# Finer regions in an ordering model: quarters of the inverse's DRAM tiles and buffers, halves of stored weights, columns of tables

## The chip, the core and the metric

The kernel runs on one core of one Trainium2 chip. The metric is the device time of one execution in microseconds. Beside it stands one execution that the hardware profiler recorded: its timeline runs from the first to the last instruction (the "span"), and it names for each group of instructions the engine, the output tile and the input tiles. The engines are PE (matrix products), PEld (PE's weight loads, which overlap it), DVE, ACT and POOL (work on rows of SBUF and PSUM), and SP, which here only issues DMAs; "SPq" is its queue. "Granted clock" is the share of PE's full speed that the profile shows as granted.

## What is computed

One decoder layer on 4096 tokens of width 1024, followed by an RMSNorm. One projection of the normalised input feeds two head groups: four heads of gated linear attention (GLA) and eight RWKV-7 heads. Their outputs, gated, are concatenated, projected and added to the input.

```python
def _rwkv7_scan(r, decay, k, v, kk, a):
    def step(S, inp):
        r_t, w_t, k_t, v_t, kk_t, a_t = inp
        sa = jnp.einsum('bhvk,bhk->bhv', S, -kk_t)
        S = (S * w_t[:, :, None, :]
             + sa[..., None] * (kk_t * a_t)[:, :, None, :]
             + v_t[..., None] * k_t[:, :, None, :])
        y = jnp.einsum('bhvk,bhk->bhv', S, r_t)
        return S, y
...
def _hybrid_layer(x, norm_w, w_in, ...):
    h = _rmsnorm(x, norm_w)
    u = (h @ w_in).astype(f32)
    gla_u, rwkv_u = u[..., :GLA_IN], u[..., GLA_IN:]
...
    o = _gla_chunked(q, k, v, log_a.reshape(B, T, GLA_HEADS, GLA_DK))
...
    y = _rwkv7_scan(r_h, decay.reshape(hs), k_h, v_h, kk, a.reshape(hs))
...
    merged = jnp.concatenate([gla_out, rwkv_out], axis=-1).astype(x.dtype)
    return x + merged @ w_out
```

The state S of an RWKV head is corrected at every token by a rank-one term that depends on S itself. The kernel takes 64 tokens at a time; within such a chunk the corrections form a triangular system, whose matrix it inverts.

## The kernel before

**Tiling.** The tokens are cut into 8 blocks of 512. In a block, the 8 RWKV heads are worked in 4 pairs; a pair in a block is a "unit", 32 in all, numbered 4 x block + pair. A unit has 8 chunks of 64 tokens. Tiles hold features on the 128 partitions and tokens along the row, so that the two heads of a pair fill the two halves of 64 partitions. Activations and weights of the large projections are split into a high and a low f16 part, and the products run as matmuls of 128x512 (`bank<-x,wr`, `bank<-x,wg`, `bank<-x,wo`).

**Streams.** Eight generators are interleaved: x (load and normalise a block), w (load the 37 weight tiles, scale them, split them into f16 halves, store each into its own DRAM tile `wdr`; the first twelve also stay in SBUF), a (`rwkv_ab`, line 862: the projections of r, k, v and the gate of a unit, on buffers `wr`), i (`rwkv_i`, line 1012), c (`rwkv_c`, line 1034), p and g (the GLA heads, on buffers `wg`) and o (`out_block`, line 1272, and `out_last` for the last block, on buffers `wo`). Both halves of a stored weight are loaded again into a `wr`, `wg` or `wo` buffer for each use: 256 KB a transfer. `absmax_scale`, with its small tile `amo`, scales the merged heads before the output projection.

**The inverse of a unit.** After the projection of r, PE makes the score products `bank<-DD,bk` (32 for a unit), and DVE copies the lower triangles into the tile `Nb`, which holds for each chunk a 128x128 square for the two heads. The square's four diagonal blocks of 32x32 are inverted on POOL, all chunks and blocks of a unit at once, with the 32 blocks laid on 128 partitions. For that layout the blocks go through DRAM and back:

```python
        F = sb(rt, [P, 1024], F32, "f4", 1).rearrange("p (k t) -> p k t", k=32)
        nd = sb(dr, [4, NC, 32, 32], F32, "nd", 2)
        for q in range(4):
            D.dma_start(nd[q].rearrange("c j i -> j c i"), nb[32 * q:32 * q + 32, :, 32 * q:32 * q + 32])
        for g in range(4):
            D.dma_start(F[32 * g:32 * g + 32].rearrange("p k t -> p (k t)"), nd.rearrange("q c j i -> (q c) (j i)"))
...
        td = sb(dr, [8, 4, 32, 32], F32, "td", 2)
        for g in range(4):
            D.dma_start(td[:, g].rearrange("m q i -> q m i"), Tc[32 * g:32 * g + 32])
        for q in range(4):
            D.dma_start(nb[32 * q:32 * q + 32, :, 32 * q:32 * q + 32],
                              td[:, :, NC * q:NC * q + NC].rearrange("m g c i -> (m g) c i"))
```

Four stores fill `nd`, a quarter each. Four loads fill `F` (in the profile "f"); each reads all of `nd` and writes 32 partitions. Between the two pieces shown, POOL solves in 31 steps of two operations on `tm` and `Tc` (DVE in the last unit). Four stores fill `td`, and four loads put the inverted blocks back into `Nb`, 32 partitions each. Then `rwkv_i` transposes (tile `Ta`) and joins the 32x32 blocks into the inverse of 64x64 by the products `bank<-Ta,Nb` and `bank<-Nb,Ta`.

**The chain.** `rwkv_c` walks the 8 chunks of a unit in turn. Each has three products that wait for one another through ACT and DVE: `ch<-sv,DD`, `ch<-us,Nb`, `ch<-uv,bk`. The y products follow. A unit's chain needs the state that the chain of the same pair left in the block before, and the chains run one after the other.

**The order.** No instruction is issued as the generators come to it. Every call of an engine passes through a helper (`Engine.call`; all instructions have its line, 438, in the profile), which gives it a modelled duration and a lag, and hands it to `put` (line 223). `put` builds a graph: a step follows the last writer of each region that it reads or writes, and the readers of each region that it writes. A follower waits in the model for the end and the lag of the step before, if the region is "timed", that is, if `parts` (line 105) names it too; otherwise only its place behind that step is kept. A DMA that stores into `nd` or `td` has a lag of 0.6 or 1.2 us, and `SPARE` adds 0.45 behind each DMA. The first pass (`account`, line 169) interleaves the streams by these times, with the same regions. Then `forward` and `backward` (lines 264 and 332) place all steps on modelled engines, in 50 passes with five settings, and the pass whose modelled end is smallest sets the order in which all instructions are issued. SP has one queue for all DMAs, in that order. What an instruction waits for on the chip does not come from this model but from its real operands.

**Regions.** `whole` (line 203) gives the regions of an operand. Before, a DRAM tile is one region, and so is a table named in `TABLES` (small tiles in which each column belongs to another weight or pair); an SBUF tile has one region for each half of 64 partitions, and some are cut further by their row. So in the model the four stores into one `nd` follow each other, each after the one before has landed; the same holds for `td`, and for the steps that write different columns of one table.

Of the kernel before, what the change touches and what calls it, by code (L numbers as in the profile page):

```python
# [18 lines left out]
DRAM = bass.MemoryType.DRAM  # L19

P = 128
DM = 1024
KT = 8
# [23 lines left out]
NC = TB // C  # L47
# [34 lines left out]
def hymba_kernel(ctx, tc, xT, wt, wg, wo, wua, gup, pk, ck, out):  # L82
# [14 lines left out]


    TABLES = ("pkt", "scl", "invs", "hinv", "mu_s", "omu_s", "carry", "wosc", "woinv", "gnh", "lnh")
    HEADS, XS = set(), set()  # L100
    now = [0.0]
    streams = []
    ready, used, busy = {}, {}, {}

    def parts(ap):
        if ap.tensor.name == out.tensor.name or ap.tensor.name.rsplit("_", 1)[0] in TABLES:
            return []
        if ap.space == DRAM:
            return [(ap.tensor.name, 0)]
        a = ap.start_partition()  # L110
        hs = range(a // 64, (a + ap.shape[0] - 1) // 64 + 1)
        if ap.tensor.name in HEADS:
            o = ap.offset % P // 64
            e = range(2) if ap.ap[-1][1] > 64 else range(o, o + 1)
            return [(ap.tensor.name, h, i) for h in hs for i in e]
        if ap.tensor.name in XS:
            o = ap.offset % (4 * TB) // TB
            e = range(o, o + max(1, math.prod(ap.shape[1:]) // TB)) if ap.dtype == F16 else range(4)
            return [(ap.tensor.name, h, 2 + i) for h in hs for i in e]
        return [(ap.tensor.name, h) for h in hs]  # L120
# [48 lines left out]
    def account(eng, out, ins, d, lag, cols=0, tiles=None):  # L169
        rdy = lambda k: (lambda r: r[0] + early(r[1], eng))(ready.get(k, (0.0, "")))  # L170
        t = max([0.0] + [rdy(k) for a in ins for k in parts(a)]
                + [used.get(k, 0.0) for k in parts(out)]
                + [rdy(k) for k in parts(out) if eng != "T"])
        if eng == "T":
            t0, d = array.put(max(t, now[0]), d, cols, tiles)
            t, now[0] = t0, array.free
        else:
            if eng == "D":
                t0 = place("H", t, 0.5)
                t = t0 + 1.15  # L180
            t = place(eng, t, d)
            if eng != "D":
                t0 = t
        for a in ins:
            for k in parts(a):
                used[k] = max(used.get(k, 0.0), t + d + (0.95 if eng == "D" else 0.1))
        for k in parts(out):
            ready[k] = (t + d + lag, eng)
        return t0
# [13 lines left out]
    def whole(ap):  # L203
        if ap.tensor.name == out.tensor.name:
            return []
        if ap.tensor.name.rsplit("_", 1)[0] in TABLES or ap.space == DRAM:
            return [(ap.tensor.name, 0)]
        return parts(ap)

    class Step:  # L210
# [12 lines left out]
    def put(t0, eng, d, lag, cols, tiles, tab, outs, ins, f):  # L223

        keys = lambda aps: {k: k in {y for x in aps for y in parts(x)} for a in aps for k in whole(a)}
        ki, ko = keys(ins), keys(outs)
        for k in list(ki) + list(ko):
# [250 lines left out]
    def sb(pool, shape, dt, tag, bufs=1):  # L478

        key = (tag, dt)  # L480
        if key not in ring:
            ring[key] = [0, [pool.tile(shape, dt, tag=f"{tag}_{i}", name=f"{tag}_{i}") for i in range(bufs)]]
        r = ring[key]
        t = r[1][r[0] % len(r[1])]
        r[0] += 1
        return t
# [32 lines left out]
    for g in range(4):  # L519
        q = slice(32 * g, 32 * g + 32)  # L520
# [38 lines left out]
    Nb = [sb(un, [P, NC, 192], F32, f"Nb{i}") for i in range(NBUF)]  # L559
# [37 lines left out]
    wdr = [dr.tile([2, P, KT, P], F16, tag=f"wdr{i}", name=f"wdr{i}") for i in range(NWT + KT)]  # L597
# [987 lines left out]
```

## Time and profile before

| | |
|---|---|
| median of 3 runs | 2355.93 us (2353.73 to 2357.6) |
| the profiled execution | 2350.84 us |
| its span | 2348.7 us |
| mean granted clock of PE | 0.982 |
| PE busy | 2230.6 us |
| HBM read, written | 276.94 MB, 45.05 MB |

The profiled execution is one of its own, a little shorter than the three timed runs; its own time is 2.1 us more than its span. Three groups of matmuls make up two thirds of PE's busy time; columns are the line, engine, operation, output and inputs, tile and shape, type and count, then busy us and mean ns of one, then the idle time of the engine before them and what ended it:

```
L438 PE MATMUL bank<-x,wr 128*128 128x512 f16 x3264 | 795.7, 381 | 13.3 <-DVE SC L438 4.7
L438 PE MATMUL bank<-x,wg 128*128 128x512 f16 x1536 | 376.9, 381 | 1.9 <-ACT bk L438 1.2
L438 PE MATMUL bank<-x,wo 128*128 128x512 f16 x1488 | 364.2, 382 | 2.2 <-DMA wr<-wdr 0.8
```

The mean of one matmul there is its own length; matmuls overlap, so that the pace at which they follow each other is read from a run of them in a timeline. Idle time is credited in such rows to the group that stands behind it, and the releaser is inferred from semaphores.

### The profile page before, as it was taken

The page shows a single profiled execution, that of the slowest core. Times are in us where ns is not written, and L with a number is a line of the kernel's source. Part 1 is how long each engine was busy: PE and PEld are TensorE (multiplying, and loading weights), DVE is VectorE, ACT ScalarE, POOL GpSimd, SP SyncE. Part 2 cuts the span into 40 slices and gives each one's busy share as a digit, 9 for nine tenths or more (in the row PEclk, how much of TensorE's full clock was granted, in tenths as well). Part 3 has the DMA queues.
Part 4 walks back from the last instruction along what each step waited for, and adds up shares of the span by engine and source line. Part 5 has one row for each costly group of instructions (what it writes and reads, how often), then busy time and mean ns, then how long its engine had stood idle before and what let it go on. Part 6 is the DMA issues. An engine that isn't in the chain of part 4 may idle for free.

```text
span 2348.7 us, 52029 instructions
## 1 busy us (share of the span) xinstructions
PE 2230.6 (95%) x19304; PEld 1365.0 (58%) x19304; DVE 1715.9 (73%) x3801; ACT 1257.4 (54%) x3229; POOL 865.6 (37%) x2212
## 2 busy tenths in 40 slices
PE   6998999899999999999999999999999999999976
PEld 2555565456665557556575556655575565755643
DVE  7977778568773886849776687748867487766756
ACT  7557765345643646545654556446464555544442
POOL 2442333524334153444524253341524446241300
PEclk9988999999999999999999999999999999999989
DMA  5685645354334642445434543346424464344432
GB/s 183 199 267 167 187 151 151 93 175 139 111 105 128 191 147 74 127 128 188 131 92 124 184 145 109 106 127 192 148 76 128 121 193 121 98 119 123 123 96 75
DMA packets 275362, 325.41 MB, mean 139 GB/s; under 512 B 131572, under 2 KB 132772, under 8 KB 275108
## 3 DMA queue, kind: packets, MB, share of 16 engines
q1 hardware_dynamic: 275108, 322.10, 45.5%
q8 instruction: 151, 2.47, 0.4%
q14 instruction: 103, 0.84, 0.1%
HBM read 276.94 MB, written 45.05 MB: 137 GB/s over the span
## 4 chain that ended last, share of the span: by engine, by line
PE 72%; DVE 14%; DMA 7%; ACT 4%; issue 2%; SPq 1%; POOL 0%; DVEq 0%; ACTq 0%; POOLq 0%
PE bank L438 63%; PE ch L438 7%; PE y L438 3%; DVE DD L438 1%; DMA wg<-wdr 1%; SPq L438 1%; DVE bk L438 1%; DVE x L438 1%; DMA rn<-bcda 1%; DVE nta L438 1%; DMA xr<-in_xT_dram 1%; ACT wo L438 1%; DVE Nb L438 1%; DMA wdr<-wo 1%; DVE mgr L438 1%
## 5 line engine op out<-in xcount | busy, mean ns | idle before, releaser
L438 PE MATMUL bank<-x,wr 128*128 128x512 f16 x3264 | 795.7, 381 | 13.3 <-DVE SC L438 4.7
L438 POOL TENSOR_TENSOR tm<-Tc,f 128x60 f32<-128x60 f32 (+24 forms) x961 | 338.3, 352 | 583.1 <-DMA f<-nd 468.1
L438 PEld LDWEIGHTS <-wr 128*128 128x128 f16 x3264 | 314.1, 100 | 314.7 <-issue 25.6
L438 POOL TENSOR_TENSOR Tc<-Tc,tm 128x60 f32<-128x60 f32 (+24 forms) x961 | 356.7, 371 | 74.6
L438 PE MATMUL bank<-x,wg 128*128 128x512 f16 x1536 | 376.9, 381 | 1.9 <-ACT bk L438 1.2
L438 PE MATMUL bank<-x,wo 128*128 128x512 f16 x1488 | 364.2, 382 | 2.2 <-DMA wr<-wdr 0.8
L438 DVE SCALAR_TENSOR_TENSOR sv<-ch,PC,psd 64x64 f32<-64x64 f32 x448 | 126.5, 282 | 217.2 <-PE ch L438 212.1
L438 POOL TENSOR_TENSOR xacc<-xacc,xr 128x512 f32<-128x512 f32 x98 | 132.7, 1354 | 344.2 <-ACT xr L438 229.5
L438 PEld LDWEIGHTS <-wg 128*128 128x128 f16 x1536 | 147.7, 100 | 149.3 <-issue 8.1
L438 PEld LDWEIGHTS <-wo 128*128 128x128 f16 x1488 | 146.2, 101 | 133.5 <-issue 4.9
L438 PE MATMUL bank<-wg,x 128*128 128x128 f16 x3072 | 197.5, 222 | 12.4 <-DMA wg<-wdr 12.3
L438 PEld LDWEIGHTS <-x 128*128 128x128 f16 x3120 | 189.6, 100 | 32.3 <-issue 20.0
L438 ACT ACTIVATE psd<-sv,PC 128x128 f32<-128x128 f32 x256 | 102.3, 400 | 180.7 <-DVE sv L438 135.2
L438 ACT COPY uv<-ch 64x64 f32<-64x64 f32 x512 | 105.8, 207 | 106.7 <-PE ch L438 100.8
L438 POOL MEMSET Tc<- 32x8 f32 (+1 forms) x160 | 23.6, 148 | 360.1 <-DMA td<-Tc 312.2
L438 ACT COPY us<-ch 64x64 f32<-64x64 f32 x512 | 105.5, 206 | 91.7 <-PE ch L438 83.5
L438 PEld LDWEIGHTS ch<-sv,DD 128*128 128x128 f32 x512 | 91.5, 192 | 41.4 <-DVE sv L438 14.9
L438 PEld LDWEIGHTS ch<-uv,bk 128*128 128x128 f32 x512 | 91.1, 192 | 41.5 <-ACT uv L438 16.1
L438 PEld LDWEIGHTS ch<-us,Nb 128*128 128x128 f32 x512 | 88.6, 192 | 44.7 <-ACT us L438 21.5
L438 ACT ACTIVATE sa<-bank,mu_s 128x512 f32<-128x512 f32 x104 | 71.6, 688 | 75.1 <-PE bank L438 74.3
L438 PE MATMUL ch<-uv,bk 128*128 128x128 f32 x512 | 105.8, 289 | 5.5 <-ACT uv L438 5.2
L438 PE MATMUL ch<-sv,DD 128*128 128x128 f32 x512 | 105.2, 288 | 4.9 <-DVE sv L438 4.7
(333 smaller groups left out, 3681.7 us busy)
## 6 DMA issues: line engine op xcount, KB each, us to landing
wr<-wdr SPq DMA_DIRECT2D x256, 256.0 KB
wg<-wdr SPq DMA_DIRECT2D x184, 256.0 KB
xr<-in_xT_dram SPq DMA_DIRECT2D x176, 256.0 KB
wo<-wdr SPq DMA_DIRECT2D x128, 256.0 KB
f<-nd SPq DMA_DIRECT2D x128, 128.0 KB
x<-in_wt_dram SPq DMA_DIRECT2D x29, 512.0 KB
wdr<-wo SPq DMA_DIRECT2D x25, 512.0 KB
out_dram<-mgg SPq DMA_DIRECT2D x33, 256.0 KB
```

The source lines that it names most:

```text
L438: put(t0, self.name, d, lag, cols, tiles, tab, outs, ins, lambda: f(*a, **kw))
```

## The change

The table of regions becomes finer. A new function `dram` gives four regions for a tile `nd` (a store touches the one that it writes, a load into F touches all four), four for `td` (again a store touches one, a load back into `Nb` all four) by their offsets, two for a stored weight `wdr` (the high and the low f16 half), and one for any other DRAM tile. `Nb` and `f` have a region for each 32 and each 16 partitions instead of 64. A table has a region for each column of its row; as before, tables are not timed.

The diff:

```diff
@@ -97,17 +97,33 @@
     TABLES = ("pkt", "scl", "invs", "hinv", "mu_s", "omu_s", "carry", "wosc", "woinv", "gnh", "lnh")
+    FINE = {"Nb": 32, "f": 16}
     HEADS, XS = set(), set()
...
+    def dram(ap):
+
+        name = ap.tensor.name
+        if name.startswith("nd"):
+            return [(name, i) for i in (range(4) if ap.shape[0] == 32 and len(ap.shape) == 2 else [ap.offset // (NC * 1024) % 4])]
+        if name.startswith("td"):
+            return [(name, i) for i in (range(4) if ap.ap[0][0] >= 1024 else [ap.offset // 1024 % 4])]
+        if name.startswith("wdr"):
+            return [(name, i) for i in ([ap.offset // (P * DM) % 2] if ap.ap[0][1] == P and len(ap.shape) == 3 and ap.shape[1] == KT and ap.shape[2] == P else range(2))]
+        return [(name, 0)]
+
     def parts(ap):
         if ap.tensor.name == out.tensor.name or ap.tensor.name.rsplit("_", 1)[0] in TABLES:
             return []
         if ap.space == DRAM:
-            return [(ap.tensor.name, 0)]
+            return dram(ap)
         a = ap.start_partition()
+        tag = ap.tensor.name.rsplit("_", 1)[0].rstrip("0123456789_")
+        if tag in FINE:
+            q = FINE[tag]
+            return [(ap.tensor.name, h) for h in range(a // q, (a + ap.shape[0] - 1) // q + 1)]
         hs = range(a // 64, (a + ap.shape[0] - 1) // 64 + 1)
@@ -203,8 +219,11 @@
     def whole(ap):
         if ap.tensor.name == out.tensor.name:
             return []
-        if ap.tensor.name.rsplit("_", 1)[0] in TABLES or ap.space == DRAM:
-            return [(ap.tensor.name, 0)]
+        if ap.space == DRAM:
+            return dram(ap)
+        if ap.tensor.name.rsplit("_", 1)[0] in TABLES:
+            w = math.prod(ap.tensor.shape[1:])
+            return [(ap.tensor.name, i) for i in range(ap.offset % w, ap.offset % w + math.prod(ap.shape[1:]))]
         return parts(ap)
```

The number of instructions of each kind is the same; the order differs on all five engines, nearly everywhere. (The lines are shifted: what was line 438 is line 457.) Three places, as the two programs issue them, follow; a number behind a tile's name is its buffer, and x4 stands for four in a row.

SP's queue in unit 10, from its first store into `nd` to its loads of F (`f_0_215`); `xr`, `wr` and `bcdx`, `xacc` are loads and broadcasts of other streams. Before:

```order
L438 DMA nd_245<-Nb_0_134 32x8x32
L438 DMA xr_221<-in_xT_dram 128x512
L438 DMA wr_214<-wdr_148 128x1024
L438 DMA xr_220<-in_xT_dram 128x512
L438 DMA nd_245<-Nb_0_134 32x8x32 x2
L438 DMA wr_211<-wdr_144 128x1024
L438 DMA wr_212<-wdr_144 128x1024
L438 DMA bcdx_275<-nyg_207 4x128
L438 DMA nd_245<-Nb_0_134 32x8x32
L438 DMA xacc_193<-bcdx_275 128x512
L438 DMA f_0_215<-nd_245 32x1024 x2
```

With the change:

```order
L457 DMA nd_245<-Nb_0_134 32x8x32 x4
L457 DMA wr_211<-wdr_144 128x1024
L457 DMA wr_212<-wdr_144 128x1024
L457 DMA bcdx_275<-nyg_207 4x128
L457 DMA f_0_215<-nd_245 32x1024 x4
L457 DMA xacc_193<-bcdx_275 128x512
```

The four stores into `nd`, which had six other transfers between them, stand side by side, and the four loads of F too.

PE near the end, where it comes to the products with Ta of unit 30 (its `Nb` is `Nb_0_134`); before, the last of the projections on `wr` stands ahead of them:

```order
L438 LDWEIGHTS wr_212
L438 MATMUL bank_0_182<-x_1_3_0_83,wr_212 128x512
L438 MATMUL bank_0_184<-ident_102,bk_242 128x128 x4
L438 MATMUL bank_0_187<-ident_102,amo_281 128x128
L438 MATMUL bank_0_185<-Ta_251,Nb_0_134 32x32 x16
L438 MATMUL bank_0_185<-Nb_0_134,Ta_251 32x32 x16
L438 MATMUL ch_266<-us_267,Nb_0_134 128x64
L438 MATMUL ch_266<-uv_133,bk_241 128x128
```

With the change:

```order
L457 MATMUL bank_0_185<-qi_243,gep_227 128x128
L457 MATMUL bank_0_186<-Ta_251,Nb_0_134 32x32
L457 LDWEIGHTS wg_230
L457 MATMUL bank_0_184<-x_1_2_0_82,wg_230 128x512
L457 MATMUL bank_0_186<-Ta_251,Nb_0_134 32x32 x15
L457 LDWEIGHTS wg_230
L457 MATMUL bank_0_184<-x_1_3_0_83,wg_230 128x512
```

These products now stand ahead of most of the last projections, whose matmuls come behind them, among the steps of the last two chains. Between the last score product of unit 31 and the first of these products stood 75 f16 matmuls of 128x512, and now 12.

PE in the chain of unit 0, about half-way. Before:

```order
L438 LDWEIGHTS wg_230
L438 MATMUL bank_0_183<-x_0_3_0_79,wg_230 128x512
L438 MATMUL ch_266<-us_267,Nb_0_134 128x64
L438 MATMUL bank_0_187<-ident_102,amW_209 128x128
L438 MATMUL ch_266<-uv_133,bk_241 128x128
L438 MATMUL ch_266<-sv_254,DD_0_131 128x128
L438 MATMUL ch_266<-us_267,Nb_0_134 128x64
```

With the change:

```order
L457 LDWEIGHTS wr_211
L457 MATMUL bank_0_186<-x_0_2_0_78,wr_211 128x512
L457 MATMUL ch_264<-sv_254,DD_0_131 128x128
L457 MATMUL bank_0_187<-rn_195,bones_98 32x128 x4
L457 MATMUL bank_0_187<-r_199,bones_98 32x128 x4
L457 LDWEIGHTS wr_211
L457 MATMUL bank_0_186<-x_0_3_0_79,wr_211 128x512
L457 MATMUL ch_264<-us_265,Nb_0_134 128x64
```

Steps of the chain that stood back to back now have matmuls of other streams between them.

## The prediction

> **What bounds the kernel now.** I read the page first (busy times, the 40 slices), then windows cut where the slices change, then the waits of PE, then the timelines of single places.
>
> ```profile
> span 2348.7 us, 52029 instructions
> PE 2230.6 (95%) x19304; PEld 1365.0 (58%) x19304; DVE 1715.9 (73%) x3801; ACT 1257.4 (54%) x3229; POOL 865.6 (37%) x2212
> PE   6998999899999999999999999999999999999976
> PEclk9988999999999999999999999999999999999989
> ```
>
> PE is busy in 95% of the span; 118.1 us are idle, mostly at the two ends. The windows put sizes to it; columns: length, busy us (instructions) of PE, PEld, DVE, ACT, POOL, then PE's granted clock, DMA share, GB/s.
>
> ```profile
> 0.00:470.00 470.00, 413.78 (x3338) 248.09 (x3339) 363.00 (x920) 289.80 (x664) 176.55 (x444) 0.95 0.57 175
> 470.00:2174.00 1704.00, 1676.82 (x14780) 1032.26 (x14779) 1235.65 (x2593) 902.32 (x2382) 665.07 (x1701) 1.00 0.44 133
> 2174.00:2219.30 45.30, 43.44 (x398) 27.50 (x395) 34.59 (x69) 19.57 (x53) 20.07 (x49) 1.00 0.48 149
> 2219.30:2252.30 33.00, 21.46 (x140) 11.38 (x139) 23.77 (x72) 7.82 (x18) 3.92 (x18) 0.90 0.37 84
> 2252.30:2263.00 10.70, 8.57 (x87) 6.85 (x88) 9.68 (x35) 6.21 (x15) 0.00 (x0) 0.50 0.09 15
> 2263.00:2318.50 55.50, 53.21 (x453) 32.00 (x452) 27.43 (x70) 25.16 (x88) 0.00 (x0) 1.00 0.31 93
> 2318.50:2348.70 30.20, 13.30 (x120) 6.94 (x120) 21.74 (x46) 6.50 (x11) 0.00 (x0) 0.82 0.19 70
> 171.00:213.00 42.00, 33.58 (x281) 23.28 (x278) 31.52 (x84) 35.84 (x88) 18.19 (x44) 0.84 0.64 193
> 405.00:446.00 41.00, 33.23 (x276) 18.11 (x276) 29.52 (x59) 16.48 (x40) 22.52 (x68) 0.88 0.30 79
> ```
>
> From 470 to 2174 PE is the bound: 1676.8 busy of 1704.0, at full clock. A new order can win at most 27 us there, and can lose much more. What can be won lies in the first 470 us (56 idle, clock 0.95) and after 2219.3 (11.5 idle, then 10.7 us at half clock, then 17 idle at the very end).
>
> ```profile
> PE bank L438 <- DVE Ta L438: 14.3, 6, 11.5
> PE bank L438 <- DMA wg<-wdr: 12.8, 7, 3.6
> PE bank L438 <- DVE amo L438: 6.6, 4, 3.4
> ```
>
> The longest wait of PE is one: 11.5 us for Ta, which the inverse feeds. Ahead of it PE has run out of matmuls; x20 also gives the pace of a 128x512 f16 matmul, (4.48 - 0.38) / 19 = 0.216 us.
>
> ```profile
> 2231.08 4.48 PE L438 MATMUL bank<-x,wr 128*128 128x512 f16 x20
> ...
> 2240.27 0.49 PE L438 MATMUL bank<-ident,amo 128*128 128x128 f32 x2
> 2252.30 0.31 PE L438 MATMUL bank<-Ta,Nb 32*32 32x32 f32 x2 [11.54 <-DVE Ta L438]
> ```
>
> **The inverse's round trip.** Unit 10, in mid-kernel, shows what the old table does to every unit. Rows of PE, SP's queue and POOL in order of time:
>
> ```profile
> 798.94 2.06 PE L438 MATMUL bank<-DD,bk 64*128 64x128 f32 x32
> 805.01 0.38 SPq L438 DMA_DIRECT2D nd<-Nb  x1
> 807.60 0.92 SPq L438 DMA_DIRECT2D nd<-Nb  x2
> 813.80 0.43 SPq L438 DMA_DIRECT2D nd<-Nb  x1
> 815.81 0.79 SPq L438 DMA_DIRECT2D f<-nd  x2
> 820.06 0.89 SPq L438 DMA_DIRECT2D f<-nd  x2
> 823.78 0.30 POOL L438 TENSOR_TENSOR tm<-Tc,f 128x31 f32<-128x31 f32 x1 [16.59 <-DMA f<-nd]
> 853.70 0.22 POOL L438 TENSOR_TENSOR Tc<-Tc,tm 128x8 f32<-128x8 f32 x1
> 854.27 0.44 SPq L438 DMA_DIRECT2D td<-Tc  x1
> 866.88 0.41 SPq L438 DMA_DIRECT2D td<-Tc  x1
> 870.72 0.86 SPq L438 DMA_DIRECT2D Nb<-td  x2
> 873.54 0.92 SPq L438 DMA_DIRECT2D Nb<-td  x2
> 877.76 0.93 PE L438 MATMUL bank<-Ta,Nb 32*32 32x32 f32 x26
> ```
>
> From the last score product (801.0) to the first product with Ta (877.8) it takes 76.8 us, and POOL's solve is only 30.1 of them. Four stores to nd are spread over 9.2 us and four to td over 13.0, because the model took nd and td for one region each and let each store wait for the one before. Nothing on the chip asks for that; where a unit has them side by side, four take about 2 us:
>
> ```profile
> 2219.84 2.18 SPq L438 DMA_DIRECT2D nd<-Nb  x4
> 2257.22 1.80 SPq L438 DMA_DIRECT2D td<-Tc  x4
> ```
>
> **The change part by part.** No instruction of work is added or removed; only positions in the five engines' orders change. (1) Quarters of nd, td, Nb and f: in the order the four stores to nd, four loads of f, four stores to td and mostly the four loads of Nb stand side by side. Unit 10 would take 76.8 - (9.2 - 2.2) - (13.0 - 1.8) - (5.1 - 1.8) = 55.3 us, the 5.1 being its f loads, put at 1.8 like td's stores. In the changed order PE also arrives sooner: 111 matmuls on wr stand between the same two points against 183, 72 x 0.216 = 15.6 us less, and some 3 us of f32 work less; 58 us against 55. So the round trip is hidden in mid-kernel as before and wins nothing there.
>
> It wins in the tail. Between the last score product of unit 31 and Ta of unit 30 stood 75 f16 matmuls (48 wr, 27 wg); now 12, and the other 63 stand behind, between the steps of the last two chains. PE gets to that Ta at about 45 us (unit 30's score products to unit 31's: the window 2174.0 to 2219.3) plus 6, so 51 to 55 us after unit 30's score products, near the 55 that the trip needs. What goes: 33.0 - 21.46 = 11.5 us of idle time, and half of the 8.57 us that PE ran at clock 0.50 behind it, 4.3; together 15.8. Zero is the other end (the wait stands elsewhere). I take 13: Ta may be 3 us late.
>
> [...]
>
> (2) Output block 0 (window 405 to 446: 7.8 idle, clock 0.88). Between the last y product of unit 3 and amo stood 24 matmuls on wr, now 47: 23 x 0.216 = 5.0 us more cover for the wait on amo (3.4 of it here). At most 7.8 + 0.12 x 41 = 12.7, at least 0; I take 5.
>
> (3) The first chain (window 171 to 213: 8.4 idle, clock 0.84). Eleven of its steps stood back to back without a matmul between them (0 or 1); now two. But at this point the stored weights, of which 512 KB go each way per weight, set the pace (DMA share 0.64), so most of the idle time can come back elsewhere. Between 0 and 8.4 + 6.7; I take 3.
>
> (4) Halves of stored weights, and loads of wg. The loads with less than 3.6 us of PE work between the matmul that frees the buffer and the one that needs it are 3, were 8; but two of them now have 2 us. Of the 12.8 us of waits I take 3 as won, between -5 (worse) and 10.
>
> (5) Columns of tables: they free small DVE and ACT steps in the first 200 us, where their share of the order is already set by weights that arrive; nothing. Changes of tile form or type on PE fall from 2232 to 2204. From one row to the next a change to f32 costs 2265.46 - 2264.21 - 5 x 0.216 = 0.17 us:
>
> ```profile
> 2264.21 1.26 PE L438 MATMUL bank<-x,wo 128*128 128x512 f16 x5
> 2265.46 0.43 PE L438 MATMUL ch<-us,Nb 128*128 128x64 f32 x2
> ```
>
> 28 of them make at most 4.8; I take 2, the least 0.
>
> (6) What it costs. Cover of the round trip shrinks in all units by 9 to 22 us (15 on average), the trip by about 21. Units 19 and 20, whose cover falls by 22 and 21, and some four more have none to spare: six stalls of 1 us, 6. The queue of SP is one, in order, and with fewer transfers between nd's stores and f's loads it stands waiting for a landing, with weight loads behind it:
>
> ```profile
> SPq L438 <- DMA td<-Tc: 25.9, 16, 3.8
> SPq L438 <- DMA nd<-Nb: 14.1, 15, 2.7
> ```
>
> 0.9 and 1.6 us a time now; for all 32 units instead of half of them that is 40 us more on the queue, nearly all behind loads that have slack; 3 on PE. Two units have the score products 5 to 6 us behind the r projection: 2. Together 11; 0 to 40 are the ends.
>
> Sum: -13 - 5 - 3 - 3 - 2 + 11 = -15. The profiled execution took 2350.84 us, 2.1 around its span of 2348.7; it would be 2336. The median shown, 2355.93, lies 5.1 above the profiled execution; I carry the 15 over: **2341 us**.
>
> **The rivals.** (A) Slower: the inverse becomes the bound. If a round trip keeps its waits for landings (the 1.6 and 0.9 above, and POOL's 3 us from f's last issue), every unit is short by a little, and PE, in order, stands at Ta. 28 units x 1.5 us = 42, against 26 of gains: 2355.93 + 16 = 2372. It decides from 26 / 28 = 0.9 us a unit. For it: the new order leaves 3 us in unit 10, and PE had no room in 470 to 2174. Against it: the model's own times for a landing fit what the trace shows (f issued 2.0 us after nd's last store), and six waits for Ta in 32 units say that its plan is kept. [...]
>
> ```profile
> 2256.34 0.69 PE L438 MATMUL ch<-us,Nb 128*128 128x64 f32 x2 [0.84 <-ACT Nb L438]
> ...
> 2284.67 0.49 PE L438 MATMUL ch<-uv,bk 128*128 128x128 f32 x2
> ```
>
> (B) The tail's wait moves: the chains of units 30 and 31 follow each other, and these rows, the first and the last of unit 30's, are 29 us apart; stores of x and wo loads stand behind the same queue; then 13 falls to 2 and the sum is -4: 2352. For it: 17 us idle at the very end are left in either order. Against it: 63 matmuls (13.6 us) now fill those chains. (C) More: the idle time of windows 171 to 213 and 405 to 446 goes wholly, 15 + 12 in place of 8, and the inverse costs half: 2341 - 19 - 5 = 2317. That the order hardly changes is excluded by the order itself: it differs nearly everywhere.
>
> **How the numbers follow.** The forecast has 0.60 (2329 to 2349), A 0.20, B 0.13, C 0.07. Likeliest 2341. The range goes down to 2322, into C, and up to 2366, into the lower half of A. About 0.2% (4.7 us) is what a measurement of this kernel can tell from no change. Faster: the forecast, C and a fifth of B, 0.70; the rest of B, 0.10, is the same; A, 0.20, slower.
>
> **What would show it.** Right: no PE wait for Ta over 4 us near the end and no half clock behind it; nd's four stores within 3 us and td's within 3 in most units; from the score products to Ta 51 to 60 us in place of unit 10's 76.8; the wait for amo in block 0 under 2 us; PE busy in the middle window as now, 98%. Wrong: waits of PE for DVE Ta above 30 us in many pieces, or for wg and wr loads above 20 (A); the same end with 11 us idle at another row (B). A weight pipeline that has become slower in the first 220 us would make it wrong in a way that I have not priced.

## The result, and the profile after

| | before | with the change |
|---|---|---|
| median (4 runs each) | 2356.76 us (2353.73 to 2359.95) | 2319.55 us (2318.72 to 2320.13) |
| the profiled execution | 2350.84 us | 2320.13 us |
| its span | 2348.7 us | 2318.4 us |
| mean granted clock in it | 0.982 | 0.988 |

The ratio of the runs is 0.9842 (0.9825 to 0.9859): 37 us faster. The forecast was 2341, with a range from 2322, and the measured time lies below that range, near rival C's 2317. The sign and the four places were right, the size was too small.

The page of the changed kernel, the same lines as before:

```profile
span 2318.4 us, 52055 instructions
PE 2225.7 (96%) x19304; PEld 1360.7 (59%) x19304; DVE 1711.3 (74%) x3801; ACT 1252.8 (54%) x3229; POOL 875.5 (38%) x2212
PE   6999999999999999999999999999999999999996
PEclk9989999999999999999999999999999999999998
```

PE is idle for 92.7 us, was 118.1; its busy time fell by only 4.9. The nines are now unbroken from the second slice to the last but one. The two windows at which the forecast hesitated, and the end, in the windows view (columns as in the prediction):

```profile
171.00:213.00 42.00, 38.87 (x454) 28.16 (x452) 38.32 (x98) 31.57 (x72) 6.81 (x20) 0.96 0.64 195
405.00:446.00 41.00, 41.00 (x271) 22.77 (x270) 17.58 (x41) 18.69 (x56) 22.58 (x75) 1.00 0.46 127
2205.00:2287.00 82.00, 76.83 (x641) 44.77 (x640) 55.04 (x172) 37.71 (x118) 0.00 (x0) 0.98 0.33 95
2287.00:2318.40 31.40, 14.35 (x117) 7.63 (x117) 20.58 (x43) 6.49 (x11) 0.00 (x0) 0.71 0.18 68
```

At the first chain PE is busy for 38.87 of 42 us (33.58 before) at clock 0.96 (0.84), at output block 0 for all 41 (33.23) at 1.00 (0.88). The last 31 us are as empty as they were. The waits of PE (in total, times, longest):

```profile
PE bank L457 <- DVE amo L457: 4.6, 3, 3.0
PE bank L457 <- DMA wg<-wdr: 3.6, 4, 2.0
PE bank L457 <- DVE Ta L457: 3.4, 5, 1.8
```

Ta 3.4 us in place of 14.3, loads of wg 3.6 in place of 12.8. Unit 10's round trip, rows of PE, SP's queue and POOL (no row of POOL in the traces of the two kernels names a tile in PSUM):

```profile
776.31 1.61 PE L457 MATMUL bank<-DD,bk 64*128 64x128 f32 x24
781.64 1.81 SPq L457 DMA_DIRECT2D nd<-Nb  x4
787.73 1.73 SPq L457 DMA_DIRECT2D f<-nd  x4
793.14 0.24 POOL L457 TENSOR_TENSOR tm<-Tc,f 128x31 f32<-128x31 f32 x1 [12.99 <-DMA f<-nd]
826.47 0.22 POOL L457 TENSOR_TENSOR Tc<-Tc,tm 128x8 f32<-128x8 f32 x1
829.83 1.88 SPq L457 DMA_DIRECT2D td<-Tc  x4
834.50 1.84 SPq L457 DMA_DIRECT2D Nb<-td  x4
840.60 0.24 PE L457 MATMUL bank<-Ta,Nb 32*32 32x32 f32 x2 [1.76 <-DVE Ta L457]
```

All four groups of transfers are issued in under 2 us each. From the last score product (777.9) to Ta it is 62.7 us in place of 76.8. That is 7 us more than the 55.3 worked out for this unit: the solve took 33.6 us in place of 30.1, and the loads of f and the stores to td were issued 2.7 and 2.8 us later behind what they wait for. Over the 32 units the median of this trip went from 70.5 to 55.8 us.

**Where the time went, by equal work.** Since the order differs everywhere, equal windows of time hold unequal work. So each matmul is counted with the median interval to the next matmul that its kind (tiles and shape) shows over all the traces, and the span is cut where these counts reach the same sums. Each row of this table then holds the same amount of matmul work in both orders; idle time is that ahead of matmuls, and "half clock" is what matmuls took beyond their count where half the clock was granted.

| stretch (start in before) | before us | after us | difference | idle | half clock |
|---|---|---|---|---|---|
| start (4) | 163.9 | 162.0 | -1.9 | 31.1 to 29.3 | 5.7 to 7.5 |
| first chain (168) | 61.7 | 50.9 | -10.8 | 8.8 to 3.1 | 5.3 to 1.6 |
| to block 0's end (230) | 161.6 | 157.7 | -3.9 | 7.5 to 3.5 | 0 to 0 |
| output block 0 (392) | 59.8 | 50.0 | -9.8 | 8.8 to 4.1 | 4.5 to 0 |
| behind it (451) | 112.1 | 108.1 | -4.0 | 3.6 to 1.5 | 2.8 to 0 |
| middle (563) | 1519.6 | 1535.4 | +15.8 | 22.1 to 28.2 | 1.3 to 4.9 |
| before the end (2083) | 112.5 | 109.1 | -3.4 | 1.5 to 0.1 | 1.6 to 0 |
| the end (2196) | 144.4 | 131.1 | -13.3 | 25.9 to 14.0 | 5.7 to 4.2 |

They add up to -31.3, against 30.3 between the spans. The other 6.5 of the 37 us is how the profiled executions stand to the medians: that of before was 6 us under its median, that of after 0.6 above. Of 19 other executions of the kernel before, 17 had a clock of 0.981 or less, the profiled one 0.982; all four of the changed kernel had 0.988 or 0.989.

### The profile page after: what moved, and what is told of

It is laid out like the page before. It is cut to its first block, busy times and chain, and to the rows that moved or that the text cites. A ratio compares the mean times of both kernels' runs of the same rounds, so it can differ in the third digit from the quotient of the medians.

```text
span 2318.4 us, 52055 instructions
## 1 busy us (share of the span) xinstructions
PE 2225.7 (96%) x19304; PEld 1360.7 (59%) x19304; DVE 1711.3 (74%) x3801; ACT 1252.8 (54%) x3229; POOL 875.5 (38%) x2212
## 4 chain that ended last, share of the span: by engine, by line
PE 65%; DVE 19%; DMA 8%; ACT 4%; issue 2%; SPq 1%; POOL 0%; DVEq 0%; ACTq 0%
PE bank L457 56%; PE ch L457 6%; PE y L457 3%; DVE DD L457 2%; DVE nta L457 2%; DMA xr<-in_xT_dram 1%; DVE x L457 1%; SPq L457 1%; DVE bk L457 1%; DVE xr L457 1%; DMA Nb<-td 1%; DVE Nb L457 1%; DVE mgg L457 1%; DMA wdr<-wo 1%; DVE mgr L457 1%
## 5 line engine op out<-in xcount | busy, mean ns | idle before, releaser
L457 POOL TENSOR_TENSOR tm<-Tc,f 128x60 f32<-128x60 f32 (+24 forms) x961 | 347.3, 361 | 719.6 <-DMA f<-nd 635.6
L457 PE MATMUL bank<-x,wo 128*128 128x512 f16 x1488 | 359.5, 380 | 0.5 <-ACT x L457 0.4
L457 PE MATMUL ch<-us,Nb 128*128 128x64 f32 x512 | 92.1, 262 | 7.2 <-ACT us L457 7.1
```

The source lines that it names most:

```text
L457: put(t0, self.name, d, lag, cols, tiles, tab, outs, ins, lambda: f(*a, **kw))
```

## The experiments

All keep the work as it is unless said otherwise, and all are variants of the two kernels. Each of the five sets below stands beside runs of the kernel before on the same chip, whose median was 2357.1, 2353.6, 2354.4, 2355.4 and 2356.0 us; the ratios go by these. Differences to the changed kernel's 2319.55 us, which comes from another set, may be off by some 3 us, as far as those medians lie apart.

### Which part of the change

Quarters of nd and td with the finer buffers (no halves, no columns):

```diff
-        if name.startswith("wdr"):
-            return [(name, i) for i in ([ap.offset // (P * DM) % 2] if ap.ap[0][1] == P and len(ap.shape) == 3 and ap.shape[1] == KT and ap.shape[2] == P else range(2))]
...
-            w = math.prod(ap.tensor.shape[1:])
-            return [(ap.tensor.name, i) for i in range(ap.offset % w, ap.offset % w + math.prod(ap.shape[1:]))]
+            return [(ap.tensor.name, 0)]
```

> Quarters of nd and td and the finer parts of Nb and f alone; stored weights and tables as before. Theory R (the shorter round trip of the inverse makes the whole gain): 2318 to 2330, the first chain (171 to 221) with 5 us less idle time than before, output block 0 without idle time, no wait for Ta over 4 us at the end. Rival W (the halves of stored weights make the gain of the first 220 us): some 10 us slower than the full change, 2330, with the idle time and the half clock of 171 to 213 as before. Rival T (table columns make it): the same 2330, told from W by the halves alone.

Measured: 2318.46 us (2312.83 to 2323.61), ratio 0.9839 (0.9818 to 0.986).

Halves of stored weights alone; from the full change, with the columns out as above:

```diff
-    FINE = {"Nb": 32, "f": 16}
+    FINE = {}
...
-        if name.startswith("nd"):
-            return [(name, i) for i in (range(4) if ap.shape[0] == 32 and len(ap.shape) == 2 else [ap.offset // (NC * 1024) % 4])]
-        if name.startswith("td"):
-            return [(name, i) for i in (range(4) if ap.ap[0][0] >= 1024 else [ap.offset // 1024 % 4])]
```

> Halves of stored weights alone. Theory R: 2352 to 2358, within 0.2% of before, with the four stores to nd spread over 9 us and the wait of PE for Ta near the end still there. Rival W: 2343 to 2348, with the gain at 171 to 213. Rival T: no change.

Measured: 2357.96 us, ratio 1.001 (0.9995 to 1.0025).

Quarters of nd and td alone, from the first variant:

```diff
-    FINE = {"Nb": 32, "f": 16}
+    FINE = {}
```

> Quarters of nd and td alone, with Nb and f in halves of 64 partitions. Theory R, if the DRAM tiles carry it: 2320 to 2332, the round trip near 58 us against 70.5 before and 55.8 with the full change. Rival B (the finer parts of the buffers carry it): 2340 or more, with loads of f still apart.

Measured: 2332.92 us, ratio 0.9899 (0.9884 to 0.9914); median trip 58.3 us.

The finer buffers alone, from the kernel before:

```diff
+    FINE = {"Nb": 32, "f": 16}
...
+        tag = ap.tensor.name.rsplit("_", 1)[0].rstrip("0123456789_")
+        if tag in FINE:
+            q = FINE[tag]
+            return [(ap.tensor.name, h) for h in range(a // q, (a + ap.shape[0] - 1) // q + 1)]
```

> Finer parts of Nb and f alone, nd and td one region each as before. Theory R: stores to nd and td still spread over 9 us each, only the loads of f and Nb close together, so 5 us off the round trip of 70.5, and a third of the gain at most: 2344 to 2352. Rival B: 2320 to 2332.

Measured: 2354.94 us, ratio 0.9994 (0.9984 to 1.0003); median trip 67.2 us, and PE's wait for Ta is still there:

```profile
PE bank L443 <- DVE Ta L443: 14.0, 11, 9.5
```

So theory R stands in the main: quarters with finer buffers reach the whole gain without halves and columns. Its ranges were missed twice, by 0.9 us for the quarters alone and by 3 for the buffers alone, which won less than R gave them. By these single orders the quarters of the DRAM tiles carry 24 us, and the buffers, worth next to nothing without them, 14 more; orders by the same rules differ by up to 20 us (next part), so this split is not settled. For the total W and T fall: halves alone win nothing in the one order tried, and with columns as the only edit the instructions come out in the old order, row for row.

In places halves and columns do leave a mark. PE waits for loads of wg 3.5 to 5.7 us in the four orders of the full rules (those of the next part and of the last run included), and 8.8 to 21.0 in the eleven others without a delay. By the count of the table above, the work that the kernel before has done at 563 us is done at 563 to 571 us in the four orders without quarters or finer buffers, at 543 to 552 in the seven that have either but no halves and columns, and at 528 to 535 in the four of the full rules. What the full rules are ahead there they lose in the middle: the first variant, some 10 us behind at that point, takes no longer in all. No run tells halves from columns in this.

### How much is the search's luck

The full change and the kernel before, with `SPARE` at other values than 0.45, for instance

```diff
-SPARE = 0.45
+SPARE = 0.46
```

> The full change, with the model's spare time behind a DMA at 0.46 in place of 0.45: the same rules, another order out of the search. Theory S (the gain beyond the forecast is systematic: the shorter round trip sets it): 2314 to 2326. Rival L (the search's luck made the difference between the forecast 15 and the measured 37): anywhere from 2320 to 2345, most likely near 2335.

Measured: 2316.7 us (2314.89 to 2318.61), ratio 0.9844 (0.983 to 0.9859).

> The full change with that spare time at 0.50. Theory S: 2314 to 2326, and mid-kernel waits for Ta and weights a little fewer than with 0.45. Rival L: 2320 to 2345.

Measured: 2318.19 us (2316.8 to 2323.21), ratio 0.9855 (0.9839 to 0.987). Waits for Ta 1.9 us in place of 3.4, for wg 3.5 in place of 3.6.

> The kernel before with that spare time at 0.46. Theory S: 2350 to 2362, with the wait for Ta near the end and half clock at the first chain still there. Rival L: off by 10 us or more from 2357 in either direction.

Measured: 2370.06 us, ratio 1.0068 (1.0051 to 1.0085).

> The kernel before with that spare time at 0.40. Theory S: 2350 to 2362. Rival L: off by 10 us or more from 2357 in either direction, where the long waits at the first chain, at output block 0 or at the end stand elsewhere.

Measured: 2373.49 us, ratio 1.0086 (1.007 to 1.0102).

The new rules give 2317 to 2320 in each of three orders: S, not L, for the change. For the kernel before it is L: its other orders are 13 and 16 us off 2357, and 16 and 20 us worse than the runs of before beside them. So 0.45 was a lucky value among the three tried; the order of halves alone, with as long a trip (median 73.1 us), also took 2358, and how far the old rules vary is not known better than that. The luck stands in the middle stretch: 1519.6 us there against 1540.7 and 1536.3 with the other two values.

The model does not see this luck. Its own end, by which each kernel chooses its order, is 2351.5 us for the kernel before and 2355.8 and 2347.8 with the two other values. For the new rules it is 2297.4, 2304.6 and 2303.9, and for the buffers alone 2323.7: 28 us that the model wins there and the chip does not.

### Which units

On the first variant, the quarters apply in some units only, for instance

```diff
-            return [(name, i) for i in (range(4) if ap.ap[0][0] >= 1024 else [ap.offset // 1024 % 4])]
+            return [(name, i) for i in (range(4) if ap.ap[0][0] >= 1024 else [ap.offset // 1024 % 4] if fine[0] else range(4))]
...
+        fine[0] = u < 2
```

and the same for nd.

> Finer buffers in all units, quarters of nd and td in units 0 and 1 only. Theory P (each place wins by its own units' round trip): the stretch of matmul work that holds the first chain takes 49 to 56 us against 62 before and 60 with the buffers alone, the end stays as with the buffers alone, in all 2342 to 2350. Rival G (a looser graph lets the search do better wherever, the place doesn't follow the units): the first chain's stretch stays near 60, or the gain stands elsewhere.

Measured: 2355.96 us, ratio 0.9998 (0.9987 to 1.0009).

> Quarters in units 2 to 5 only. Theory P: the first chain's stretch near 60 as before, that of output block 0 50 to 53 us against 60 before (54.5 with the buffers alone), the end as before, in all 2345 to 2355. Rival G: no such order of places.

Measured: 2359.02 us, ratio 1.0014 (1.0 to 1.0029).

> Quarters in units 6 to 27 only, the middle of the kernel. Theory P: nothing to win there, since the round trip was hidden: first chain near 60 and the end near 150 us as before, in all 2350 to 2362. If the shorter trip without slack costs in the middle, as forecast, 2360 to 2372. Rival G: 2320 to 2340, as much as from quarters everywhere.

Measured: 2323.7 us, ratio 0.9864 (0.9848 to 0.988).

> Quarters in units 28 to 31 only. Theory P: no wait for Ta over 4 us near the end, the last stretch 137 to 141 us against 150 before, the first chain near 60 as before, in all 2338 to 2348. Rival G: gains at the first chain too, or the wait for Ta still there.

Measured: 2338.06 us, ratio 0.9923 (0.9903 to 0.9943).

Stretches of equal work in these four, one profiled execution each, us:

| quarters in units | first chain | output block 0 | middle | the end |
|---|---|---|---|---|
| none, finer buffers alone | 60.3 | 54.4 | 1545.1 | 143.1 |
| 0, 1 | 47.7 | 55.7 | 1542.8 | 142.5 |
| 2 to 5 | 65.0 | 54.2 | 1529.8 | 142.3 |
| 6 to 27 | 62.3 | 49.8 | 1523.0 | 138.3 |
| 28 to 31 | 56.9 | 53.0 | 1528.5 | 137.1 |
| all (first variant) | 48.7 | 54.3 | 1523.3 | 130.4 |

P holds at one place and in part at another. The first chain is short only where units 0 and 1 have quarters: 47.7 to 55.5 over seven such orders, 56.9 to 67.4 over the eight others of this study. The end is 130.4 to 138.4 with quarters in units 28 to 31 against 138.3 to 146.5 without; but 138.3 is the order with quarters in units 6 to 27, where the longest wait for Ta is 0.6 us, so the long wait can go without quarters in the end's own units. P fails at output block 0, which is as long with quarters in units 2 to 5 as without any (54.2 and 54.4) and shortest with quarters in units 6 to 27. It fails in the middle, where I expected nothing to win, and 2323.7 is G's number: quarters there take 22 us off what the buffers alone gave. Not all of the 22 can be theirs, since two orders without quarters in the middle come to 1529.8 and 1528.5.

Of P's totals the first three missed. What units 0 and 1 won at the first chain was lost in the stretches behind it: against the buffers alone that chain is 12.6 us shorter, but the work that before has done at 563 us ends at the same time (544.6 and 544.3). The fourth total, 2338.06, lies in P's range for another reason: of what it wins on the buffers alone, 16.6 us stand in the middle and 6.0 at the end. So the runs by units show where a shorter trip shows first, not that each place's gain reaches the total.

### The trip itself, with the order held

POOL's first product of the solve is issued again, with the same result; the model does not know of it, so PE's order stays row for row:

```diff
+            if j == 0 and (u in (0, 1)):
+                steps[-1].again = 64
...
             s.f()
+            for _ in range(getattr(s, "again", 0)):
+                s.f()
```

> The full change in its own order, with POOL's first product of the solve repeated 64 times in units 0 and 1 (same result), which makes each of the two round trips some 20 us longer. Theory D (at the first chain the round trip itself is on the path, with 2 to 3 us to spare): 15 to 35 us more, 2335 to 2355, all of it in the stretch of the first chain. Rival O (the new order carries the gain, the trip is covered there): under 5 us more, 2319 to 2325.

Measured: 2358.18 us, 38.6 more than the full change, where the two solves became 25 us longer each. It is outside D's range, 15 us of it stand ahead of the first chain's stretch, and the path was another than expected. Rows of POOL, SP's queue, ACT and PE in unit 0:

```profile
92.21 32.52 POOL L457 TENSOR_TENSOR tm<-Tc,f 128x31 f32<-128x31 f32 x65 [12.54 <-DMA f<-nd]
130.74 0.38 SPq L457 DMA_DIRECT2D nd<-Nb  x1
150.57 1.78 SPq L457 DMA_DIRECT2D td<-Tc  x4
152.94 0.40 SPq L457 DMA_DIRECT2D wdr<-wo  x1
156.27 1.06 ACT L457 ACTIVATE wo<-x 128x1024 f32<-128x1024 f32 x1 [18.34 <-DMA wdr<-wo]
157.47 0.79 PE L457 MATMUL bank<-ident,amW 128*128 128x128 f32 x2 [15.87 <-ACT wo L457]
```

SP issues nothing from 131.1 to 150.6, because the stores to td at its head wait for POOL. Behind them stands the store of a weight (`wdr<-wo`), ACT waits for the buffer that it frees, and PE waits for the weight's scale, before it comes to Ta at all. The same happens in unit 1 (16.9 us). So this run shows what a late solve costs here through the queue; how much time Ta itself has to spare it does not show.

> The same repetition in unit 3 only, whose chain ends ahead of output block 0. Theory D: its trip has under 1 us to spare, so 15 to 22 us more, 2335 to 2342, at the stretches from unit 3's Ta to output block 0. Rival O: under 5 us more.

Measured: 2338.99 us, 19.4 more, in one wait; the solve became 23.7 us longer:

```profile
361.92 0.31 PE L457 MATMUL bank<-Ta,Nb 32*32 32x32 f32 x2 [18.75 <-DVE Ta L457]
```

> The same product repeated 14 times in units 6 to 27, some 4 us a unit. Theory J (just in time: in the new order the trips of the middle end when PE arrives, about half of them with less than 1.5 us to spare): 30 to 50 us more, 2350 to 2370, as waits of PE for Ta. Rival C (cover is left, as the 3.4 us of waits for Ta in all suggest): under 12 us more, 2319 to 2332.

Measured: 2373.23 us, 53.7 more for some 4.3 us of POOL's work a unit, by which the solve, from its first step to its last, became 5.5 us longer on average. Of the 58 us by which the middle stretch is longer in the profiled execution, 35 are idle time of PE and 18 half clock; the waits for Ta are 24 of the 35:

```profile
PE bank L457 <- DVE Ta L457: 27.4, 21, 6.4
```

> The repetition of 64 in unit 30 only. Theory D: nothing to spare, the old wait for Ta is back with about 15 to 20 us and half clock behind it, 2335 to 2345. Rival O: under 5 us more.

Measured: 2335.22 us, 15.7 more, in one wait; the solve became 20.8 us longer:

```profile
2217.12 0.31 PE L457 MATMUL bank<-Ta,Nb 32*32 32x32 f32 x2 [16.12 <-DVE DD L457]
```

Ta itself was written 0.8 us before this row starts; the last of the wait is DVE's next step, on DD.

D holds in units 3 and 30, where some 5 us of the longer solve found cover. In units 0 and 1 it missed the range and the path. J's direction holds in the middle; the loss is 3 us above its range, and the waits for Ta are less than half of it. O and C fall everywhere. The same delay in the middle of the old order:

> The kernel before in its own order, with the same 14 repetitions in units 6 to 27 as in the run on the full change's middle, which lost 54 us. Theory J (both orders are just in time: the search holds back exactly as many matmuls as the trip needs, so the change made the trip cheaper, not tighter): 40 to 60 us more, 2396 to 2417. Rival T (the old order had cover to spare and the new one is tighter, as the forecast's 11 us took it): under 25 us more, 2357 to 2380.

Measured: 2400.14 us, ratio 1.0179 (1.0147 to 1.0212), 44 more, for solves 5.1 us longer on average. The old order was nearly as tight as the new one; T falls. Here most of the new idle time does not stand at Ta but is spread over loads of wg and a dozen others:

```profile
PE bank L438 <- DMA wg<-wdr: 20.7, 11, 3.5
PE bank L438 <- DVE Ta L438: 20.3, 10, 11.5
```

Before the delay these were 12.8 and 14.3 us.

At last the full change with another search. The first of the five settings is the one whose passes hold the best modelled end (2297.4; the best of the other four is 2309.8). It gets 20 passes, and the other four are left out, so that there are 20 passes in all in place of 50:

```diff
-        for keep, look in ((0.5, 0.15), (0.5, 0.3), (0.7, 0.3), (1.0, 0.15), (2.0, 0.3)):
+        for keep, look in ((0.5, 0.15),):
...
-            for _ in range(10):
+            for _ in range(20):
```

> The full change with 20 passes of the search's first setting in place of 10 passes of each of the five. Theory S (the rules set the time, the search's rest is luck of a few us): 2312 to 2324, within the spread of the three orders of these rules so far. Rival L (more search still pays): under 2312.

Measured: 2311.46 us (2309.16 to 2317.07), ratio 0.9816 (0.9789 to 0.9842). It is 8 us below the changed kernel, all its runs lie below that kernel's lowest, and it is the fastest of the study. By its median it is L's, by half a microsecond, and its highest run lies in S's range. The modelled end is 2293.5, 3.9 us lower. More passes of this setting may pay a few us; no more is shown.

## Why the forecast fell short

**Term (1), the trip and the end, was right in its mechanism and, partly by luck, in its number.** The trip was put at 51 to 60 us and its median is 55.8, though unit 10's is 62.7; unit 30's was put at 51 to 55 and is 53.1. The end was put at 13 us and won 13.3. Its wait came back, at 16.1 us, as soon as the trip of unit 30 was made longer. But the parts differ: idle time fell by 11.9 us and half clock by only 1.5, where I had 11.5 and 4.3 and took some 3 off for a late Ta. The half clock behind Ta is gone; other half clock stands at 2228 and in the last 31 us, whose clock fell from 0.82 to 0.71.

Of the half clock behind the old wait I counted 4.3 us, half of what PE was busy in 10.7 us at 0.50. How long half clock lasts behind a wait is not the same everywhere. Behind the 18.75 us wait in unit 3 PE was busy for 3.38 of 3.40 us at 0.50, and the next 6.7 us show 0.96.

```profile
361.90:365.30 3.40, 3.38 (x37) 1.66 (x38) 2.94 (x5) 1.50 (x5) 0.00 (x0) 0.50 0.81 285
365.30:372.00 6.70, 6.70 (x71) 4.01 (x70) 5.30 (x13) 2.76 (x11) 0.00 (x0) 0.96 0.57 168
```

Behind the old wait the half clock lasted longer. In the traces of the two kernels all changes of the granted clock are whole multiples of 3.413 us apart. Cut by this step, before shows PE busy for 2.12 and then 2.65 of 3.40 us, with the clock still at 0.50, and 0.99 behind the first stretch that is busy throughout:

```profile
2252.70:2256.10 3.40, 2.12 (x62) 1.85 (x62) 2.99 (x15) 0.54 (x2) 0.00 (x0) 0.50 0.00 0
2256.10:2259.50 3.40, 2.65 (x9) 2.14 (x10) 3.29 (x15) 2.58 (x7) 0.00 (x0) 0.50 0.21 35
2259.50:2262.90 3.40, 3.40 (x14) 2.59 (x14) 3.03 (x5) 2.98 (x8) 0.00 (x0) 0.50 0.08 11
2262.90:2266.30 3.40, 3.40 (x19) 1.70 (x18) 2.70 (x5) 2.29 (x8) 0.00 (x0) 0.99 0.09 15
```

So the 4.3 us belong to this place: of the 10.7 us, 6.8 are two steps in which PE was busy for 62% and 78%, and 3.4 one in which it was busy throughout.

**Terms (2) and (3) were mis-sized, and this is the step that failed.** Output block 0 was given 5 of at most 12.7 us and won 9.8; the first chain 3 of at most 15.1 and won 10.8. I had both ends from the windows and took a low value each time. At block 0 I priced only the 23 more matmuls ahead of amo (5.0 us); the wait for amo did shrink, from 3.4 to 1.15 us. At the first chain I wrote that the stored weights set the pace there, so that the idle time would come back elsewhere. In this order it did not: behind it the next stretch won 3.9 more, though the last raw weight was issued only 6 us earlier (193 against 199). Unit 0's chain starts 21 us earlier (150.7 against 172.1), since the trips of units 0 and 1 went from 92.2 and 93.2 us to 70.8 and 67.7. It ends 11 us earlier (194.1 against 205.4) and found other matmuls to stand between its steps. In two orders without halves and columns, the first variant and the one with quarters in units 0 and 1, the gain did come back as I had argued: they are at the end of the first 563 us where the buffers alone are. The runs by units show that these two trips carry the first chain; by which of their two ways, Ta or the queue of SP, is not separated. For block 0 the cause is not settled: its time moves with the order, whichever units have quarters, and the 19.4 us of the delay in unit 3 show only that the trip ahead of it has little to spare.

The balance, in the profiled execution: 15 us were forecast, the table has 31.3. Terms (2) and (3) won 12.6 more than they were given. The four other stretches, for which no term stood but the 5 us of (4) and (5), won 13.2, so 8.2 more. The middle cost 4.8 more than term (6) had. That makes 16 of the 22 us between the forecast 15 and the measured 37; the other 6 are the carry-over.

**Term (6) had nearly the right number and the wrong reason.** I charged 11 us for cover lost in the middle; the middle is 15.8 us longer. Idle time is 6.1 of the 15.8 and half clock 3.6; the rest stands in neither column. PE waits for Ta only 3.4 us there and everywhere, and for weights less than before. The old order was nearly as tight (44 us lost to the delay, 53.7 in the new), and the old middle was an exception: 1519.6 us, where the seven other orders without quarters in the middle have 1528.5 to 1545.1 and the seven with them 1523.0 to 1535.4. So what was lost looks like a lucky order, not cover. That "the round trip is hidden in mid-kernel and wins nothing there" was true against this one order; against the seven others it cannot be told, since the two ranges overlap.

**The carry-over failed too.** I added the 5.1 us by which the median of before stood above its profiled execution. They did not carry over: the profiled execution of before was a short one with a high clock, that of the changed kernel an ordinary one. In 19 executions of before the clock varied from 0.977 to 0.984, and the longer ones have the lower clocks (correlation -0.74). What lets one order meet different clocks from run to run is not shown, with one trace of each.

**The rivals.** A (the inverse becomes the bound, 2372) needed 0.9 us a unit of stall; there was 0.1. B (the end's wait moves) fell: the last 31 us are as idle as they were, the rest was won. C had nearly the right number and the right places, the windows 171 to 213 and 405 to 446, but in part by luck: the two won 20.6 us where C had 27, the middle cost more and not half, and stretches that C did not name and the carry-over made up for it. Term (4) had waits for wg fall by 3 us; they fell by 9.2. Neither that nor (5) shows in a total.

What joins these: the search holds back as many matmuls as the trip needs, in each of 32 units, whichever rules it has. A trip shorter by 15 us sets some 70 matmuls free, at 0.216 us each. In the middle PE had work anyway (busy for 98% in either order), and no gain is shown there; at the first chain and at the end it stood bare, and there they count. That this is how the search uses them is argued from the orders and the places, not shown by a run of its own. Rival G, that a looser graph lets the search do better wherever, is not excluded: quarters in units 6 to 27 alone win nearly as much as quarters everywhere.

## What to carry to other kernels

Where a planner sets the order, ask first whether its model has waits that the chip has not: transfers that it spaces out, one region for a tile written in four parts. Price a shorter latency not at the units where it is hidden but at the places where the busiest engine runs out of work, and there take the idle time with the half clock behind it as the likely gain (here 5.7 and 3.7 us at the first chain, 4.7 and 4.5 at output block 0), unless a row shows what else would hold it. Compare rules over several orders each (here by one constant changed in the second digit), since a single order of the old rules was 16 to 20 us better than its two neighbours; against those the gain is 53 us, not 37. And do not take the planner's own end for a price: it fell by 28 us for the finer buffers alone, which won nothing on the chip.

## What the runs showed that I had not expected

- A late solve on POOL reached PE through SP's queue: 19 us without an issue, then a wait of 15.9 us for a weight's scale, in a place where Ta was not yet due.
- Some 4.3 us more work for POOL in each of 22 units cost 44 to 54 us, in the new order a third of it half clock (18 of 58 in the stretch) rather than idle time.
- Half clock was also granted behind waits of under 1 us: ahead of the half clock from 191.0 to 204.7 in before stand 3.4 us in which PE was busy for 1.74, with no wait above 0.74. In the traces of the two kernels the clock fell to half 20 times, each time behind 3.41 us with PE busy for at most 60%, and came back from it 18 times, each time behind 3.41 us with PE busy for at least 82%. Not every busy stretch brought it back: from 119.1 to 122.5 with the change PE was busy for all 3.40 us, and the next 6.8 us still show 0.50.
- Finer buffers alone shorten the trip from 70.5 to 67.2 us and win nothing; on top of the quarters they win 14 us, in one order of each.
